# Row sums inside r's projection, kk and v in separate buffers, and the second half's tokens fetched early, in a hybrid RWKV-7 / GLA layer

## The chip, the cores and the metric

The kernel runs on one core of one Trainium2 chip. Its time is the device time of one execution in microseconds; a kernel is judged by the median of its runs. One execution is recorded by the hardware profiler, and all rows below come from that one. TensorE multiplies matrices, VectorE and GpSimd work element by element, ScalarE evaluates functions and copies, and SyncE (SP) issues the transfers.

## What is computed

One layer of a decoder is applied to 1024 prompt tokens and to 32 sample tokens (8 sequences of 4). The residual stream, 1024 wide, goes through one input projection whose columns feed two groups of heads: RWKV-7 (8 heads of 64) and gated linear attention, GLA (4 heads). Both outputs go through an output projection and a layer norm, then a gated convolutional feed-forward and a second layer norm. The part that matters here is how RWKV-7 gets its key direction:

```python
xs = pa + (prev - pa) * mu
r, k, v, w_lo, a_lo, g_lo = split_cols(xs, [A_WIDTH, A_WIDTH, A_WIDTH, A_DECAY_LORA, A_AAA_LORA, A_GATE_LORA])
...
kk = heads(k * k_k)
kk = kk * lax.rsqrt(jnp.maximum(jnp.sum(kk * kk, -1, keepdims=True), 1e-24))
k = k * (1.0 + (a - 1.0) * k_a)
...
def step(S, inp):
    r_t, d_t, k_t, v_t, kk_t, a_t = inp
    sa = jnp.einsum('bhvk,bhk->bhv', S, -kk_t)
    S = (S * d_t[:, :, None, :] + sa[..., None] * (kk_t * a_t)[:, :, None, :]
         + v_t[..., None] * k_t[:, :, None, :])
    return S, jnp.einsum('bhvk,bhk->bhv', S, r_t)
```

kk is k scaled per head to unit length. It needs the sum of squares over a head's 64 channels, which lie on partitions, so a matmul makes the sums.

## The kernel before

**Stages.** The tokens are worked in two halves: the first holds 512 prompt tokens and the 32 sample tokens (544 columns), the second 512 prompt tokens. For each half `load_x` (line 800) brings the tokens in as eight tiles of 128 tokens by 512 channels (ten in the first half), transposes them on TensorE and splits them into a high part xh and a low part xl. Every projection (`gemm`, line 231) then makes three matmuls for each of 8 blocks of channels: 24 for a block of tokens. The first half has two blocks of 272 columns, the second one of 512. The result lands in one of two PSUM banks of the pool pg ("g" in the profile), and is evicted from there. The weights are split in the same way in `win_tile` (line 220): ScalarE casts the high part (line 225), GpSimd subtracts for the low part (line 227). Raw, high and low parts have three buffers each, and a projection takes two of each.

**Pairs.** RWKV-7 works on pairs of heads, four to a half, so Q0 to Q7. `rwkv_prep` (line 847) makes a pair's factors in this order: the projection of k with the low-rank parts of decay and in-context rate between its matmuls (lines 856 to 863, 882); the squares sq of k (line 886, ScalarE); the projection of r (line 888); the row sums of sq on TensorE and their inverse root by three Newton steps on VectorE (`pair_rsqrt`, lines 889 and 264 to 292, steps in lines 282 to 286, with a copy on ScalarE in line 290); kk from k and the transposed roots (line 898); ba = kk x a on GpSimd (line 908); the scaled factors ar (lines 910, 917) and bk (lines 920, 923) on VectorE; the projection of v (line 930), evicted by ScalarE in line 778 and corrected for the previous token by VectorE in line 772. `post` (line 938) then makes the score matrices from ar and bk (matmuls of line 943, masked in line 945), transposes bk, and forms the bonus and the transposed v.

**Buffers.** The tags e1, e3 and e4 of the pool p2 have one buffer each. In a pair e1 holds in turn sw, sq and ba, and e4 holds kk and then v. The buffers of GLA (e2, gep, sg and others) lie in the pool pl; fl, the low-rank input of GLA's decay, has a buffer in p2.

**Order.** The program is written by generators that `weave` (line 187) advances by a planned TensorE time: streams (`stream_r` for RWKV-7, `stream_g` for GLA, `stream_w` for the output projection) are taken one at a time by priority, chains (`chain_p` for post, `chain_i`, `chain_c`, `chain_t` for the recurrence, `chain_g` for GLA's) are slipped in when due. Events such as "G0" (the GLA projections of the first half are issued) or "P3" (post of Q3 is issued) hold a generator back. Order of writing is a priority: the compiler then orders each engine's queue by what its own model takes to be ready, so the trace can show instructions of a queue in another order than written, and once compiled each queue runs in order. SP's transfers are such a queue too.

**Between the halves.** `stream_r` waits for "G0" and calls `load_x` for the second half. Its eight tiles go into the buffers of raw, high and low weight parts in turn (line 809), all of them issued in `load_x`; a planned pause of 3 us follows (line 815), then the transposes. `gla_f` (line 974) follows with small weights (fraw) in the raw buffers, and `half_start` (line 829) once "P3" is there. A GLA pair ends in `gla_chain` (line 632): its last steps read the buffers sg and write the output (lines 690 to 703).

Of the kernel before, what the change touches and what calls it, by code (L numbers as in the profile page):

```python
# [9 lines left out]
F32 = mybir.dt.float32  # L10
# [7 lines left out]
P = 128  # L18
# [25 lines left out]
def step_kernel(  # L44
# [8 lines left out]
    act, dve, pool, sp = nc.scalar, nc.vector, nc.gpsimd, nc.sync  # L53
# [23 lines left out]
    pe = TensorE()  # L77
# [5 lines left out]
    def rtok(t0):  # L83
        return x_prompt[0, t0:t0 + P, :] if t0 < NP else x_sample.rearrange("b t d -> (b t) d")
# [48 lines left out]
    p2 = cx.enter_context(tc.tile_pool(name="p2", bufs=1))  # L133
    px = cx.enter_context(tc.tile_pool(name="px", bufs=1))
# [52 lines left out]
    def weave(chains, streams):  # L187
        chains, streams = [Thread(c) for c in chains], [Thread(c) for c in streams]
        cur, slot = None, 0.0
        while any(t.alive for t in chains + streams):  # L190
            live = [c for c in chains if c.ready()]
            due = [c for c in live if c.due <= pe.t]
            off = [c for c in due if not c.pe]
            if off:
                off[0].step()
                continue
            if cur is None or cur.free:
                cur = min((t for t in streams if t.ready()), key=lambda t: t.prio, default=None)
            if due and (pe.t - slot >= SLOT or cur is None or not cur.ready()):
                for c in due:  # L200
                    if c.ready():
                        c.step()
                slot = pe.t
                continue
            if cur is not None and cur.ready():
                cur.step()
                continue
            due = [c.due for c in live] + [t.blocked for t in streams if isinstance(t.blocked, float)]
            assert due, [(t.alive, t.blocked) for t in chains + streams]
            pe.t = min(due)  # L210
# [77 lines left out]
    def pair_rsqrt(sq, n, *ops):  # L288
        y = rows_rsqrt([(sq, sel2, 0)], n, *ops)
        act.copy(sq[:, 0:512].rearrange("p (a c) -> p a c", c=64), y[:, 0:8].unsqueeze(2).to_broadcast([P, 8, 64]))  # L290
        return y
# [474 lines left out]
    def shifted(H, c0, xs, ws=None):  # L766
        ft = c0 // P
        ws = ws or win_tile(c0)
        mu, halo_ = col(V_MU + ft), halo[:, ft:ft + 1]

        def add_prev(out, prev):
            dve.scalar_tensor_tensor(out, prev, mu, out, ALU.mult, ALU.add)
        for s, e in H.blocks:
            ps = gtile()
            yield from gemm(ps, ws, s, e)
            ep = min(e, 512)
            m = ep - s
            act.activation(xs[:, s:e], ps[:, 0:e - s], AF.Identity, scale=omu[:, ft:ft + 1])
            add_prev(xs[:, s + 1:ep], ps[:, 0:m - 1])
            add_prev(xs[:, s:s + 1], halo_)  # L780
            dve.tensor_copy(halo_ if H.base + ep < NP else nsh[:, ft, 0:1], ps[:, m - 1:m])
            if e > 512:
                pv, xv = s3(ps[:, 512 - s:544 - s]), s3(xs[:, 512:544])
                add_prev(xv[:, :, 1:], pv[:, :, 0:NS - 1])
                add_prev(xv[:, :, 0], sst[:, ft, :])
                dve.tensor_copy(nsh[:, ft, 1:9], pv[:, :, NS - 1])
# [9 lines left out]
    def take(gen, n):  # L796
        for _, item in zip(range(n), gen):
            yield item

    def load_x(H, between=None):  # L800
        tiles = []
        for g in range(2):
            for t0 in range(0, H.n, P):
                w, i = min(P, H.n - t0), len(tiles)
                if H.sam:
                    xt = (px.tile([P, 512], F32, name="xt", tag=("wh", "wl")[i // 3], bufs=3) if i < 6 else
                          p2.tile([P, 512], F32, name="xt", tag=("e1", "e3", "e4", "fl")[i - 6]))
                else:
                    tag, bufs = (("wraw", 3), ("wh", 3), ("wl", 3))[i % 3]
                    xt = px.tile([P, 512], F32, name="xt", tag=tag, bufs=bufs)  # L810
                sp.dma_start(xt[:w, :], rtok(H.base + t0 if t0 < 512 else NP)[:, 512 * g:512 * g + 512])
                tiles.append((t0, w, g, xt))
            if between:
                between(4 * g)
        yield ("until", pe.t + 3.0)
        for i, (t0, w, g, xt) in enumerate(tiles):
            if i % 2 == 0 or i > 3 and not H.sam:
                ps = ttile()
            else:
                ps = gtile() if i < 4 else otile("og" if i % 4 == 1 else "o")  # L820
            for j in range(4):
                pe.transpose(ps[:, j * P:j * P + w], xt[:w, j * P:(j + 1) * P], ident[:w, :w])
            src = ps.rearrange("p (j t) -> p j t", j=4)[:, :, :w]
            act.copy(xh[:, 4 * g:4 * g + 4, t0:t0 + w], src)
            dve.tensor_tensor(xl[:, 4 * g:4 * g + 4, t0:t0 + w], src,
                              f(xh[:, 4 * g:4 * g + 4, t0:t0 + w]), ALU.subtract)
            yield 0.5
# [19 lines left out]
    def rwkv_prep(Q):  # L847
# [37 lines left out]
        sq = p2.tile([P, 544], F32, name="sq", tag="e1")  # L885
        act.activation(sq[:, 0:n], k[:, 0:n], AF.Square, scale=col(V_KK + p))
        rr = s1([P, 544], "r", 3)
        yield from shifted(H, pc0, rr)
        y = pair_rsqrt(sq, n, 1e-24, 0.0, ALU.max, ALU.add)
        if Q.i >= 2:  # L890
            yield ("wait", f"C{Q.i - 2}")
        Q.E = rr_.tile([P, 8, 2, 2, CH], F32, name="E", tag="E", bufs=2)
# [1 line left out]
        Q.bkT = rr_.tile([P, 8, P], F32, name="bkT", tag="bkT", bufs=2)  # L894
        Q.ar = ars[Q.i % 2]
        Q.bon = rr_.tile([P, 512], F32, name="bon", tag="bon", bufs=2)
        kk = p2.tile([P, 544], F32, name="kk", tag="e4")
        dve.scalar_tensor_tensor(kk[:, 0:512], k[:, 0:512], col(V_KK + p), pair_spread(sq), ALU.mult, ALU.mult)
        if sam:
            ps = ttile()  # L900
# [3 lines left out]
            dve.scalar_tensor_tensor(kk[:, 512:544], k[:, 512:544], col(V_KK + p), ps[:, 0:32], ALU.mult, ALU.mult)  # L904
        arp = Q.ar
        bk = rr_.tile([P, 8, 2, CH], F32, name="bk", tag="bk")
        ba = p2.tile([P, 544], F32, name="ba", tag="e1")
        pool.tensor_tensor(ba[:, 0:n], kk[:, 0:n], aa[:, 0:n], ALU.mult)
        for h in range(2):
            dve.scalar_tensor_tensor(arp[own[h], :, 0, 1 - h, :], c3(kk)[own[h]], -1.0, pp[own[h], :, 0:CH],  # L910
# [314 lines left out]
    def chain_c():  # L1225
        for Q in Qs:
            yield ("wait", f"P{Q.i}")
            yield 1.0
            rwkv_values(Q)
            yield ("wait", f"I{Q.i}")  # L1230
            if Q.i >= 2:
                yield ("wait", f"T{Q.i - 2}")
            yield ("off", 1.0)
            yield from rwkv_chunks(Q)
            yield ("done", f"C{Q.i}")

    def chain_p():
        for Q in Qs:
            yield ("wait", f"R{Q.i}")
            if Q.i >= 2:  # L1240
                yield ("wait", f"T{Q.i - 2}")
            yield max(0.0, Q.t + POST - pe.t)
            yield from Q.post
            yield ("done", f"P{Q.i}")

    def chain_i():
        for Q in Qs:
            yield ("wait", f"P{Q.i}")
            yield 3.0
            yield from rwkv_inverse(Q)  # L1250
            yield ("done", f"I{Q.i}")

    def chain_t():
        for Q in Qs:
            yield ("wait", f"C{Q.i}")
            yield from rwkv_tail(Q)
            yield ("done", f"T{Q.i}")

    def chain_g():
        for hf, H in enumerate(Hs):  # L1260
            for g in range(2):
                yield ("wait", f"Q{hf}{g}")
                yield 2.0
                yield from gla_chain(g, hf, H.st[g])
                for q in range(2):
                    if (1, 2)[q] == 2 * hf + g:
                        yield ("wait", "P3")
                        yield ("wait", "C7" if hf * g else "P3")
                        yield from rwkv_samples(q)
                yield ("done", f"D{hf}{g}")  # L1270

    def stream_r():
        for hf, H in enumerate(Hs):
            if hf:
                yield ("wait", "G0")
                yield from load_x(H)
                yield ("done", "X1")
            yield ("wait", "lock")
            yield from half_start(H, *([] if hf else [ws0]))
            yield ("free", "lock")  # L1280
            if hf == 0:
                constants()
                yield ("done", "X0")
            for Q in Qs[4 * hf:4 * hf + 4]:
                yield ("prio", R_PRIO[Q.i])
                yield ("wait", "lock")
                yield from rwkv_prep(Q)
                yield ("free", "lock")
# [254 lines left out]
    def wpost(t0, w, xz):  # L1543
        x1, xo = (W.xa, t0) if t0 < 512 else (W.xb, t0 - 512)
        for g in range(2):
# [9 lines left out]
                act.activation(W.yc[:, 4 * g:4 * g + 4, t0 - T0:t0 - T0 + w], pv, AF.Copy, scale=ALPHA)  # L1555
            yield 0.5

    weave([chain_g(), chain_p(), chain_c(), chain_i(), chain_t()],
          [stream_r(), delay_posts(stream_w()), stream_g()])
    xa, xb, cvec, sct, f0 = W.xa, W.xb, W.cvec, W.sct, W.f0  # L1560
    wop.close()
# [195 lines left out]
```

## Time and profile before

| | us |
|---|---|
| three timed runs | 1653.04, 1675.87, 1679.36 |
| their median | 1675.87 |
| the profiled execution | 1657.51 |
| its span, first to last instruction | 1655.8 |

The span is what the rows count from: a start of 282.49 is 282.49 us after the first instruction. "Busy" of an engine is the time in which it ran an instruction. In a row of the timeline the bracket tells how long the engine had been idle before it and which instruction ended the wait.

### The profile page before, as it was taken

How to read it: one execution, taken by the hardware profiler on the slowest of the kernel's cores; microseconds unless marked ns; L12 is line 12 of the kernel's file. 1: busy time of each engine (PE TensorE's matmuls, PEld its weight loads, DVE VectorE, ACT ScalarE, POOL GpSimd, SP SyncE). 2: the span in 40 equal slices, each digit the busy share in tenths (PEclk: the TensorE clock that was granted, in tenths of full speed). 3: DMA queues.
4: the chain of work that ended last, by engine and by line, in shares of the span. 5: the costliest groups of instructions: out<-in, count | busy, mean ns of one | idle time of the engine just before them, and what ended most of it. 6: DMA issues, size and time to landing. Idle time of an engine off the chain costs nothing.

```text
span 1655.8 us, 28781 instructions
## 1 busy us (share of the span) xinstructions
PE 1570.6 (95%) x11728; PEld 1324.3 (80%) x11728; DVE 945.6 (57%) x2083; ACT 529.4 (32%) x986; POOL 358.7 (22%) x583
## 2 busy tenths in 40 slices
PE   7899889889999999998999999999999999999997
PEld 6788777766676667666878898898988889888996
DVE  4566567676787767536774444544445443454348
ACT  4453443435444435344223131221202212121222
POOL 5434424323444343331000000000000000000005
PEclk9999998989999989999999999999999999999999
DMA  4122122131211013232313020210202112021102
GB/s 140 47 65 65 39 65 71 34 85 33 59 39 46 27 46 103 79 105 87 100 43 102 26 64 27 64 52 27 64 25 65 45 34 64 14 77 43 48 27 106
DMA packets 138572, 97.36 MB, mean 59 GB/s; under 512 B 15963, under 2 KB 127003, under 8 KB 138440
## 3 DMA queue, kind: packets, MB, share of 16 engines
q1 hardware_dynamic: 138440, 95.52, 19.5%
q8 instruction: 92, 1.51, 0.4%
q14 instruction: 40, 0.33, 0.1%
HBM read 84.36 MB, written 11.15 MB: 58 GB/s over the span
## 4 chain that ended last, share of the span: by engine, by line
PE 60%; DVE 5%; issue 2%; ACT 1%; POOL 1%; DMA 1%; DVEq 0%; POOLq 0%; ACTq 0%
PE g L71 26%; PE t L71 18%; PE dn L71 13%; PE t L75 1%; PE opso L71 1%; PE sps L71 1%; PE opsog L71 1%; DVE st L1485 0%; PE up L71 0%; DVE rst L285 0%; DVE yt L1665 0%; DVE ya L1642 0%; DVE tm L327 0%; DVE yt L1666 0%; PE rp L71 0%
## 5 line engine op out<-in xcount | busy, mean ns | idle before, releaser
L71 PE MATMUL g<-xh,wh 128*128 128x272 f32 (+1 forms) x624 | 221.3, 355 | 9.5 <-DVE sg L1094 3.5
L71 PE MATMUL g<-xh,wl 128*128 128x272 f32 (+1 forms) x624 | 215.2, 345 | 3.2 <-POOL wl L227 3.2
L71 PE MATMUL g<-xl,wh 128*128 128x272 f32 (+1 forms) x624 | 216.2, 347 | 0.0
L1458 DVE TENSOR_TENSOR wlu<-wraw,whu 128x1024 fp32r<-128x1024 f32 x45 | 55.1, 1224 | 229.2 <-ACT whu L1453 220.2
L227 POOL TENSOR_TENSOR wl<-wraw,wh 128x512 fp32r<-128x512 f32 x104 | 136.3, 1313 | 168.8 <-ACT wh L225 154.2
L1607 POOL COPY ncv<-gp 128x2 f32<-128x2 f32 x22 | 20.6, 936 | 610.1 <-ACT gp L1599 610.1
L71 PEld LDWEIGHTS g<-xh,wh 128*128 128x128 f32 x624 | 122.0, 196 | 22.6 <-issue 7.0
L71 PEld LDWEIGHTS g<-xh,wl 128*128 128x128 f32 x624 | 122.2, 196 | 11.4 <-POOL wl L227 3.7
L71 PE MATMUL g<-xb,whu 128*128 128x288 f32 (+1 forms) x688 | 130.9, 288 | 0.0
L71 PE MATMUL t<-xb,whu 128*128 128x256 f32 (+1 forms) x688 | 130.5, 288 | 0.0
L71 PEld LDWEIGHTS g<-xl,wh 128*128 128x128 f32 x624 | 122.3, 196 | 9.0 <-issue 3.3
L71 PEld LDWEIGHTS t<-xb,whu 128*128 128x128 f32 x688 | 109.7, 189 | 1.8
L71 PEld LDWEIGHTS g<-xb,whu 128*128 128x128 f32 x688 | 109.7, 189 | 1.8
L71 PE MATMUL t<-xa,whu 128*128 128x512 f32 x352 | 110.2, 394 | 0.0
L225 ACT CAST wh<-wraw 128x512 fp32r<-128x512 f32 x104 | 64.0, 618 | 131.1 <-PE g L71 79.3
L71 PE MATMUL g<-xa,whu 128*128 128x512 f32 x336 | 105.6, 395 | 0.0
L1642 DVE TENSOR_TENSOR ya<-ya,dn 128x512 f32<-128x512 f32 x108 | 73.3, 684 | 53.7 <-PE dn L71 53.7
L71 PE MATMUL g<-xb,wlu 128*128 128x256 f32 (+1 forms) x344 | 99.3, 289 | 0.0
L71 PE MATMUL t<-xb,wlu 128*128 128x256 f32 (+1 forms) x344 | 99.2, 288 | 0.0
L71 PE MATMUL dn<-whd,hh 128*128 128x512 f32 x240 | 94.9, 395 | 0.0
L71 PE MATMUL dn<-wld,hh 128*128 128x512 f32 x240 | 94.6, 394 | 0.0
L71 PE MATMUL dn<-whd,hl 128*128 128x512 f32 x240 | 94.3, 393 | 0.0
(515 smaller groups left out, 3518.9 us busy)
## 6 DMA issues: line engine op xcount, KB each, us to landing
wraw<-in_w_in_dram SPq DMA_DIRECT2D x104, 256.0 KB
wraw<-in_w_up_dram SPq DMA_DIRECT2D x43, 512.0 KB
wraw<-in_w_down_dram SPq DMA_DIRECT2D x22, 512.0 KB
xt<-in_x_prompt_dram SPq DMA_DIRECT2D x16, 256.0 KB
woraw<-in_w_out_dram SPq DMA_DIRECT2D x7, 512.0 KB
ob<-od SPq DMA_DIRECT2D x7, 512.0 KB
out_dram<-yt SPq DMA_DIRECT2D x6, 512.0 KB
ya<-in_x_prompt_dram SPq DMA_DIRECT2D x5, 512.0 KB
```

Of the source, the lines that this page charges most:

```text
L71: return nc.tensor.matmul(out, lhsT, rhs, **kw)
L75: return nc.tensor.transpose(out, in_, idn)
L225: act.copy(wh, raw)
L227: pool.tensor_tensor(wl, raw, f(wh), ALU.subtract)
L1458: dve.tensor_tensor(wl, raw, f(wh), ALU.subtract)
L1607: pool.tensor_copy(ncv[:, i, 0:2], gp[:, 1024:1026])
L1642: dve.tensor_tensor(y[:, cs], y[:, cs], ps, ALU.add)
```

## The change

Three things are changed. In `rwkv_prep` the projection of r is interrupted after 24 matmuls (12 in the second half), the row sums and their inverse root are issued there, and the projection goes on. kk moves to e1 and ba is made in place in aa's buffer, so that e4 holds v alone. A new chain `fetch_x` waits until the first half's second GLA pair is finished (a new event "F01"), and issues the loads of the first five x tiles of the second half into e2, gep, both sg and fl; `load_x` then issues only the last three, all into raw weight buffers, after waiting for the fetch to be issued ("XP"), and leaves out the planned pause.

```diff
+    def fetch_x():
+        yield ("wait", "F01")
+        H1.xt = []
+        for i in range(5):
+            tag, bufs = (("e2", 1), ("gep", 1), ("sg", 2), ("sg", 2), ("fl", 1))[i]
+            xt = (p2 if i == 4 else pl).tile([P, 512], F32, name="xt", tag=tag, bufs=bufs)
+            sp.dma_start(xt, rtok(512 + P * (i % 4))[:, 512 * (i // 4):512 * (i // 4) + 512])
+            H1.xt.append(xt)
+        yield ("done", "XP")
+
     def load_x(H, between=None):
@@
+                elif i < 5:
+                    tiles.append((t0, w, g, H.xt[i]))
+                    continue
                 else:
-                    tag, bufs = (("wraw", 3), ("wh", 3), ("wl", 3))[i % 3]
-                    xt = px.tile([P, 512], F32, name="xt", tag=tag, bufs=bufs)
+                    xt = px.tile([P, 512], F32, name="xt", tag="wraw", bufs=3)
@@
-        yield ("until", pe.t + 3.0)
+        if H.sam:
+            yield ("until", pe.t + 3.0)
@@
         rr = s1([P, 544], "r", 3)
-        yield from shifted(H, pc0, rr)
+        main = shifted(H, pc0, rr)
+        yield from take(main, 24 if sam else 12)
         y = pair_rsqrt(sq, n, 1e-24, 0.0, ALU.max, ALU.add)
+        yield from main
@@
-        kk = p2.tile([P, 544], F32, name="kk", tag="e4")
+        kk = p2.tile([P, 544], F32, name="kk", tag="e1")
@@
-        ba = p2.tile([P, 544], F32, name="ba", tag="e1")
+        ba = aa
@@
                 yield from gla_chain(g, hf, H.st[g])
+                yield ("done", f"F{hf}{g}")
@@
                 yield ("wait", "G0")
+                yield ("wait", "XP")
                 yield from load_x(H)
@@
-    weave([chain_g(), chain_p(), chain_c(), chain_i(), chain_t()],
+    weave([chain_g(), chain_p(), chain_c(), chain_i(), chain_t(), fetch_x()],
```

## Rows read from the trace of the kernel before

**Rows 1.** The page: busy time of each engine, share of the span, instructions.
```profile
PE 1570.6 (95%) x11728; PEld 1324.3 (80%) x11728; DVE 945.6 (57%) x2083; ACT 529.4 (32%) x986; POOL 358.7 (22%) x583
```

**Rows 2.** Stretches: length, busy by engine (instructions), granted clock, DMA share, GB/s.
```profile
57.00:66.00 9.00, 5.23 (x25) 3.98 (x24) 7.90 (x18) 1.48 (x3) 3.74 (x5) 0.71 0.22 58
...
168.00:178.00 10.00, 6.33 (x33) 4.88 (x32) 7.92 (x21) 1.49 (x3) 4.09 (x7) 0.83 0.26 79
...
283.50:298.50 15.00, 11.57 (x101) 10.48 (x101) 13.14 (x40) 2.71 (x5) 8.33 (x11) 1.00 0.26 76
...
335.30:349.50 14.20, 9.43 (x72) 8.46 (x71) 14.04 (x50) 2.56 (x5) 2.94 (x3) 0.93 0.38 114
...
353.00:362.00 9.00, 9.00 (x37) 5.95 (x37) 4.93 (x9) 4.96 (x11) 3.30 (x5) 0.74 0.33 89
```

**Rows 3.** Timeline of TensorE: start, length, instruction, idle time before and its end.
```profile
60.12 0.43 PE L71 MATMUL rp<-srw,ar 128*128 128x64 f32 x2 [1.64 <-DVE ar L910]
62.69 0.76 PE L71 MATMUL t<-ar,bk 128*128 128x256 f32 x1 [2.13 <-DVE bk L920]
...
173.60 1.19 PE L71 MATMUL t<-ar,bk 128*128 128x256 f32 x2 [3.67 <-DVE gosb L695]
...
298.48 0.67 PE L71 MATMUL t<-ar,bk 128*128 128x256 f32 x2 [3.43 <-DVE gosb L695]
...
348.67 1.08 PE L75 MATMUL g<-ident,xt 128*128 128x128 f32 x4 [4.16 <-issue]
...
487.43 1.12 PE L75 MATMUL t<-ident,sq 128*128 128x128 f32 x4 [2.93 <-ACT sq L290]
...
585.44 0.74 PE L71 MATMUL opso<-E,UV 128*64 128x64 f32 x18 [1.94 <-POOL UV L454]
```

**Rows 4.** Timeline of the third pair (Q2), all engines, by engine.
```profile
282.49 1.23 PE L71 MATMUL t<-sel,sq 128*128 128x64 f32 x10
...
294.02 0.29 PE L71 MATMUL g<-xl,wh 128*128 128x272 f32 x1
294.14 0.29 PE L71 MATMUL g<-xh,wl 128*128 128x272 f32 x1
...
291.72 0.75 DVE L898 SCALAR_TENSOR_TENSOR kk<-k,vec,t 128x512 f32<-128x512 f32 x1 [0.40 <-PE t L75]
...
292.54 2.43 DVE L910 SCALAR_TENSOR_TENSOR ar<-kk,pp 64x512 f32<-64x512 f32 x2
...
295.11 2.35 DVE L920 TENSOR_TENSOR bk<-ba,cum 64x512 f32<-64x512 f32 x2
...
297.59 0.74 DVE L695 SCALAR_TENSOR_TENSOR gosb<-t,hng,sg 128x512 f32<-128x512 f32 x1
...
295.29 0.87 ACT L778 ACTIVATE v<-g,omu 128x272 f32<-128x272 f32 x2
...
295.38 1.54 POOL L227 TENSOR_TENSOR wl<-wraw,wh 128x512 fp32r<-128x512 f32 x1
```

**Rows 5.** Timeline of TensorE: first and last of r's last 24 matmuls, third pair.
```profile
277.89 0.43 PE L71 MATMUL g<-xh,wh 128*128 128x272 f32 x1
...
282.28 0.37 PE L71 MATMUL g<-xh,wl 128*128 128x272 f32 x1
```

**Rows 6.** The tile rst: min/median/max of a Newton step; then the fifth pair's timeline.
```profile
L284 DVE SCALAR_TENSOR_TENSOR rst<-rst x60: 148/166/1247, 52.9 to 769.6; 128x8 f32<-128x8 f32 x42, 128x10 f32<-128x10 f32 x12, 128x9 f32<-128x9 f32 x6
...
430.07 1.28 POOL L227 TENSOR_TENSOR wl<-wraw,wh 128x512 fp32r<-128x512 f32 x1
430.18 1.20 DVE L284 SCALAR_TENSOR_TENSOR rst<-rst 128x8 f32<-128x8 f32 x1
```

**Rows 7.** Timelines of SP and TensorE around the loads of the second half.
```profile
292.60 4.71 SPq L217 DMA_DIRECT2D wraw<-in_w_in_dram  x2
...
341.40 0.29 PE L71 MATMUL g<-xh,wl 128*128 128x272 f32 x1
...
352.18 0.60 PE L71 MATMUL g<-xh,fwh 128*32 128x512 f32 x1 [0.72 <-ACT xh L824]
```

## The prediction

> **What bounds the kernel now.** I read the page first for the whole, then the stretches, then the timeline of TensorE, then one hole of it on all engines. On the page TensorE is busy for 1570.6 us, 95% of the span, VectorE for 945.6, 57% [rows 1]: this is a kernel bound by TensorE, and a change pays only where TensorE stands idle or runs at the lower clock. The profiled execution took 1657.5 us, 1.7 more than its span of 1655.8. Everything that the change touches lies before 755 us.
>
> In the timeline of TensorE the idle times with the largest numbers behind a pair's v projection are of one kind [rows 3]: 1.64 and 2.13 us at the first pair, 3.67 at the second, 3.43 at the third, 4.16 at the fourth, and in the second half 2.93 at the sixth and 1.94 at the eighth. The reader is to see what ends them: a product made from kk (ar, bk), an instruction queued on VectorE behind such products (gosb, line 695), or nothing named ("issue") where a PSUM bank was missing.
>
> The third pair shows the mechanism [rows 4]. The row sums of k squared begin on TensorE at 282.49, after the whole of r's projection. Their inverse root takes VectorE and ScalarE until kk can be made at 291.72, ar from 292.54 to 294.97, and only then, at 295.29, does ScalarE evict v, because v is to lie in kk's buffer and kk's readers must be through. Until v is evicted both banks of the projections are full, so no further projection can start, and the scores of this pair need bk, which ends at 297.46. TensorE waits until 298.48. So two things end last in turn: the chain from the row sums to bk, and the bank that v holds.
>
> After these holes the clock is low: the granted share is 0.71 from 57 to 66, 0.83 from 168 to 178, 0.93 from 335.3 to 349.5 and 0.74 from 353 to 362 [rows 2]. With two levels, full and half, that is 2 x (1 - share) x length of half clock: 5.2, 3.4, 2.0 and 4.7 us. A matmul of 272 columns took 0.43 us in such a stretch and 0.29 at the full level [rows 4, 5].
>
> **The change part by part.** *Row sums amid r's projection.* No instruction is added. The ten row-sum matmuls (eight in the second half) and what hangs on them are issued after 24 of 48 matmuls, in the second half after 12 of 24. In the third pair the first and the last of those 24 start at 277.89 and 282.28 and the sums begin at 282.49 [rows 4, 5]: the chain starts 4.6 us earlier. The square of k must be there by then; it needs only the end of k's projection. Where it is late, TensorE's queue stands in front of the sums, and the rest of r's projection behind them.
>
> *Buffers of kk and v apart.* kk takes the place of its own squares (e1), ba that of aa, v alone keeps e4. Same instructions, same sizes. v's eviction then waits for its projection alone: in the third pair it can come when the last matmul of v is through, 294.4, for the first block earlier still, and a bank is free for the next projection. What becomes late next is the second half of the next weights: their low part is made on GpSimd from 295.38 to 296.92 [rows 4], because it waits for a slot that v's projection still reads. The first half of those weights feeds 12 matmuls, 12 x 0.125 = 1.5 us at the spacing of the last two v matmuls [rows 4], from 294.4 to 295.9. That leaves about 1.0 us of hole. I take 1.0 at each of the four pairs of the first half.
> Sum over these: 1.64 + 2.13 + 3.67 + 3.43 + 4.16 = 15.0, less 4.0, is 11.0 us gained. The bounds of this term are 15.0 (next projection always ready) and 0 (VectorE, busy 13.14 of 15.0 and 14.04 of 14.2 us there [rows 2], keeps the banks anyway). I stand nearer to the upper end because VectorE has no work that only these holes could hold: over the span it is 57% busy [rows 1], and the Newton steps move to where r's projection runs.
>
> *Second half.* There one projection fills one bank, and the waits come from ScalarE and VectorE queues that serve the chunk chains too. Of 2.93 + 1.94 = 4.9 us I take half, 2.4; bounds 0 and 4.9.
>
> *Clock.* The four stretches hold 15.3 us of half clock. Work there takes 0.43 for 0.29, so a third of the time, 5.1 us, is given back if no hole is left. The stretches behind the two holes of the second half I put at half as much again, an estimate. Of 7.7 I take 4.2, since holes of 1 us stay; bounds 0 and 7.7.
>
> *Tokens loaded early.* Five of eight x tiles are fetched after the first half's last GLA pair into places that are then unused; three go to the weights' raw slots. The same eight transfers are issued by SP, five earlier. The fourth pair's v matmuls end at 341.7 and the transposes' hole ended on a bank, not on a transfer [rows 3, 7]; so by itself this is worth nothing (0 to 2 us), but it covers the gain above: with the bank free at 342, tiles issued at the end of v's projection would be late. It moves one thing the wrong way: the weights of the GLA decay (fraw) follow in the raw slots, and those now hold x tiles 6 to 8 instead of 1, 4 and 7. Before, the first matmul with them started at 352.18, 10.8 us behind the last of v at 341.40 [rows 7]. Without the bank's 4.16 us that would be 6.6. Now the load waits for the sixth tile's transposes; I put the five tiles ahead of it and its own at 3.7 us, and load, cast and subtraction at 3 more, both estimates from how this stretch ran before: 6.7. A tie, cost 0 (bounds 0 and 3). The planner's pause of 3 us ahead of the transposes only orders instructions; I cost it at nothing.
>
> Sum: 11.0 + 2.4 + 4.2 = 17.6 us, from 1657.5 to 1639.9.
>
> The profiled execution lies 18.4 us below the median of the three runs, 1675.87; with it, four executions are known: 1653.0, 1657.5, 1675.9, 1679.4, whose middle is 1666.7, 9.2 above the profile. A median of the changed kernel should fall around that middle less the gain: 1639.9 + 9.2 = 1649.
>
> **The rivals.**
> *VectorE takes the gain back.* The newton steps land where GpSimd splits v's weights. A step that takes 0.17 us in the median took 1.20 beside such a split, which ran for 1.28 [rows 6]. If two of them per pair meet the Newton steps, 2 x 1.03 = 2.1 us, so the chain comes 2.5 instead of 4.6 us earlier, and r's own evictions queue behind it: some 1.5 us before v's projection at four pairs. Then 6 us of the 17.6 go, and most of the clock's share, 4: gain 7.6, 1650 on the profile's execution, 1659 at the middle. For it: VectorE at 14.04 of 14.2 us around the fourth pair [rows 2]. Against: the 57% over the span [rows 1].
> The Trainium skill ("SBUF — State Buffer", section "Who interferes with whom") says that a VectorE instruction with two SBUF inputs contends with a GpSimd one that reads SBUF and that the loser is blocked for the whole instruction. The trace agrees in the rows named. If every pair lost two full splits on TensorE's path, 8 x 2 x 1.28 = 20 us, the sum would be 1660 instead of 1639.9; no row shows that they would be on the path.
> *Only the buffers act.* The row sums come no earlier on TensorE, since k's square is late or the compiled order puts them back. Then v's eviction still frees the bank, but scores wait for bk: I give it 10 us, 1647.5, 1657 at the middle.
> *Everything closes.* 15.0 + 4.9 + 7.7 = 27.6: 1630, 1639 at the middle.
> *Slower.* SP's queue is in order. If the early x loads stand in it before the raw weights issued at 292.60 [rows 7], they hold these up until the sg buffers are read by the gosb product, 297.59 + 0.74 = 298.3 [rows 4]: the third and fourth pair's weights come 5.7 us late, the half clock behind such a hole costs 1 to 2, the fraw loads behind the last x tiles up to 3; nothing else gained, it is +10: 1667.5, 1677 at the middle. It decides once a load of x is issued ahead of those weights. Against: the gosb product itself moves earlier with the kk chain, and five loads are few.
>
> **How the numbers follow.** Forecast 0.52, VectorE 0.24, buffers alone 0.10, everything 0.06, slower 0.08. The executions known scatter by 13 us to either side of their middle, more than the cases differ: the range reaches from 1639 less about 11, 1628, to the buffers' and VectorE's case plus that scatter, 1672. A measurement of this kernel tells about 2%, 33 us, from no change; the cases end between -28 and +10, so only scatter on top of the best ones passes it: faster 0.09, within 2% 0.88, slower 0.03.
>
> **What would show it.** Right: in the timeline v's evictions start within 1 us of v's last matmul; the Newton steps run before the last matmul of r; holes behind v's projection are about 1 us; the clock shares of [rows 2] rise to 0.95 or more; the x tiles' issues on SP stand before 310. Wrong: TensorE's idle time before 780 us falls by less than 8 us, or holes of 2 us and more stand between r's and v's projection, or weights are waited for around 300.

## The result and the profile after

The changed kernel took 1672.13 us (median of 20 runs, 1657.35 to 1684.53), the kernel before, on the same chip, 1658.95 (20 runs, 1650.06 to 1679.36): a ratio of 1.0077, 95% interval 1.0055 to 1.0098. The ratios, here and below, leave out executions more than 1.5% above the fastest of their kernel, so they can differ a little from the quotient of the medians. The changed kernel is slower by 0.8%, where 1649 had been forecast: the sign was wrong, and the time lies just outside the range. The profiled execution of the changed kernel took 1669.06 us, its span is 1667.3.

What was meant to happen on the engines happened. The timeline of TensorE, of ScalarE and of VectorE for the third pair of the changed kernel answers to [rows 4]:

```profile
276.26 1.78 PE L71 MATMUL t<-sel,sq 128*128 128x64 f32 x10
277.97 0.40 PE L71 MATMUL g<-xh,wh 128*128 128x272 f32 x1
...
292.52 0.70 PE L71 MATMUL t<-ar,bk 128*128 128x256 f32 x2
...
288.96 0.49 ACT L778 ACTIVATE v<-g,omu 128x272 f32<-128x272 f32 x1 [5.50 <-PE g L71]
...
281.47 0.45 DVE L284 SCALAR_TENSOR_TENSOR rst<-rst 128x10 f32<-128x10 f32 x1
...
285.30 0.74 DVE L914 SCALAR_TENSOR_TENSOR kk<-k,vec,t 128x512 f32<-128x512 f32 x1
...
289.59 1.38 DVE L936 TENSOR_TENSOR bk<-aa,cum 64x512 f32<-64x512 f32 x2
```

The row sums stand amid r's projection, kk is made while TensorE still projects, v is evicted at 288.96 on "PE g", its own projection, and the scores at 292.52 wait for nothing. The hole of 3.43 us at this pair is gone. Other holes are there now, in the timeline of TensorE of the changed kernel:

```profile
51.72 0.55 PE L75 MATMUL t<-ident,sq 128*128 128x128 f32 x3 [1.79 <-ACT sq L290]
...
61.41 0.29 PE L71 MATMUL g<-xh,fwh 128*32 128x272 f32 x1 [1.51 <-DVE halo L781]
...
166.46 0.43 PE L71 MATMUL sps<-RU,bkT 128*128 128x64 f32 x2 [2.71 <-DVE RU L448]
...
339.63 0.63 PE L75 MATMUL g<-ident,xt 128*128 128x128 f32 x4 [0.90 <-ACT xh L838]
...
353.66 0.70 PE L71 MATMUL t<-ar,bk 128*128 128x256 f32 x2 [1.74 <-DVE E L961]
...
477.76 0.66 PE L75 MATMUL t<-ident,sqo 128*128 128x128 f32 x4 [3.58 <-ACT sqo L290]
```

Of the five holes of the first half, 15.0 us, more than half comes back as waits for something else: the inverse root itself (sq), the copy of a projection's last column (halo), a step of the recurrence (RU), the masked scores of the fourth pair (E). In the second half the hole of 2.93 us gave way to one of 3.58 that ends on another norm's inverse root (sqo). The windows of both kernels, with the columns of [rows 2], show the balance. Before:

```profile
0.00:780.00 780.00, 703.84 (x6722) 561.07 (x6723) 506.03 (x1377) 337.21 (x636) 307.09 (x479) 0.95 0.23 63
780.00:1655.80 875.80, 866.73 (x5007) 763.20 (x5006) 439.60 (x706) 192.16 (x350) 51.62 (x104) 1.00 0.17 55
...
689.00:725.00 36.00, 35.39 (x251) 24.04 (x250) 12.38 (x40) 10.91 (x22) 15.14 (x26) 1.00 0.31 81
```

After:

```profile
0.00:780.00 780.00, 708.79 (x6701) 562.63 (x6702) 501.35 (x1366) 334.83 (x631) 302.63 (x477) 0.94 0.22 61
780.00:1667.30 887.30, 874.07 (x5029) 767.83 (x5027) 444.88 (x717) 194.22 (x355) 53.68 (x106) 0.99 0.18 56
...
689.00:725.00 36.00, 36.00 (x144) 22.73 (x144) 8.09 (x25) 7.30 (x16) 8.43 (x13) 0.51 0.18 50
```

Length less busy time is TensorE's idle time: up to 780 us it was 76.2 and is 71.2. That is 5.0 us less, where the prediction called itself wrong below 8. Part of it is only late: the changed kernel is by then some 10 us behind in its work, and behind 780 it idles for 13.2 us instead of 9.1. Over the whole span the idle time is 85.2 before and 84.4 after, 0.8 less, and the same 11728 matmuls keep TensorE busy for 12.3 us longer. The loss is in busy time, not in waiting.

One row shows where: from 689 to 725 TensorE is busy for 36.00 of 36.00 us at a granted clock of 0.51, where before had 1.00. That is an unbroken stretch at the half level. Two pairs of lines from the timelines of TensorE measure it. In that place the second rwkv_samples (line 493) runs its small matmuls between the projections of the last GLA pair; its last transposes of "nat" and its first of "s0t" bound it. Before, then after:

```profile
682.88 1.06 PE L75 MATMUL t<-ident,nat 128*128 128x128 f32 x4
...
692.16 0.39 PE L71 MATMUL g<-xl,wh 128*128 128x512 f32 x1
...
711.30 0.66 PE L75 MATMUL t<-ident,s0t 128*128 128x128 f32 x4
```

```profile
680.65 0.60 PE L75 MATMUL t<-ident,nat 128*128 128x128 f32 x4
...
692.70 0.63 PE L71 MATMUL g<-xl,wh 128*128 128x512 f32 x1
...
723.57 1.11 PE L75 MATMUL t<-ident,s0t 128*128 128x128 f32 x4
```

28.42 us became 42.92. The changed kernel enters this phase 2.2 us ahead and leaves it 12.3 behind; a projection matmul takes 0.63 us in it instead of 0.39.

One number is used from here on. Every execution's record has its span and its mean granted clock; with two levels, h = 2 x span x (1 - clock) is its time at the half clock. Over the 85 executions of the kernel before that ran beside the first eleven experiments, the time follows h: 1619.8 + 0.407 h, correlation 0.99, rest 1.2 us. So h, which runs from 62 to 151 us in them, carries nearly all of this kernel's scatter. Its median is 99.5 before (98 executions, those beside the twelfth among them; the twenty of the result have no clock on record) and 123.7 after. That difference, 24.2 x 0.407, is 9.8 of the 13.2 us lost.

### The profile page after: what moved, and what is told of

It is laid out like the page before. It is cut to its first block, busy times and chain, and to the rows that moved or that the text cites. A ratio compares the mean times of both kernels' runs of the same rounds, so it can differ in the third digit from the quotient of the medians.

```text
span 1667.3 us, 28766 instructions
## 1 busy us (share of the span) xinstructions
PE 1582.9 (95%) x11728; PEld 1330.5 (80%) x11728; DVE 946.2 (57%) x2083; ACT 529.1 (32%) x986; POOL 356.3 (21%) x583
## 4 chain that ended last, share of the span: by engine, by line
PE 66%; DVE 7%; issue 2%; ACT 1%; POOL 1%; DMA 1%; DVEq 0%; ACTq 0%; POOLq 0%
PE g L71 29%; PE t L71 19%; PE dn L71 12%; PE t L75 2%; PE opsog L71 1%; PE opso L71 1%; PE sps L71 1%; PE up L71 1%; DVE tm L327 1%; PE rp L71 1%; DVE rst L285 0%; DVE bk L936 0%; DVE st L1503 0%; DVE yt L1683 0%; DVE ya L1660 0%
## 5 line engine op out<-in xcount | busy, mean ns | idle before, releaser
L71 PE MATMUL g<-xh,wl 128*128 128x272 f32 (+1 forms) x624 | 219.0, 351 | 2.8 <-POOL wl L227 2.8
```

The lines of the kernel that those rows point to most:

```text
L71: return nc.tensor.matmul(out, lhsT, rhs, **kw)
```

## The experiments

**Which part brings it?** Theory A: the long stretch at the half clock, which one part's new order brings, eats the gain. B: in the second half VectorE's Newton steps stand ahead of the recurrence. C: the early tokens cost time on SP's queue. The four kernels take parts of the change.

e1_buffers:
```
-        kk = p2.tile([P, 544], F32, name="kk", tag="e4")
+        kk = p2.tile([P, 544], F32, name="kk", tag="e1")
@@
-        ba = p2.tile([P, 544], F32, name="ba", tag="e1")
+        ba = aa
```


> Only kk into e1 and ba into aa; row sums and token loads as before. Theory A (the lost time is half clock in the last GLA pair, where small sample matmuls and projections alternate, and any new order of the queue can bring it): the holes behind v's projection in the first half shrink, the eighth pair's kk comes 5 us or more earlier, and a stretch of 20 us or more of half clock stands between 680 and 730; time 1660 to 1675. Rival B (VectorE: the Newton steps ahead of the recurrence in the second half lose the time): without the moved row sums the gain of the first half stays, 1645 to 1652. Rival C (the early tokens shift the second half): also 1645 to 1652.

e2_rows:
```
-        yield from shifted(H, pc0, rr)
+        main = shifted(H, pc0, rr)
+        yield from take(main, 24 if sam else 12)
         y = pair_rsqrt(sq, n, 1e-24, 0.0, ALU.max, ALU.add)
+        yield from main
```


> Only the row sums amid r's projection; kk, ba, v and tokens as before. Theory A: the order of TensorE changes little, no long half clock after 680, holes behind v stay at 2 us or more because v waits for kk's readers; 1652 to 1660, no different from before. Rival B: the loss shows here too, 1663 to 1672. Rival C: below before by some 5 us.

e3_tokens is the changed kernel with both of these edits undone; e4_rows_buffers is the kernel before with both, so without the early tokens.

> Only the early tokens, the event and the missing pause; rwkv_prep as before. Theory A: order of TensorE nearly as before, so the clock as before; the hole of 4.16 us ahead of the transposes stays since it waits for v's bank; 1655 to 1661. Rival B: 1655 to 1661 as well. Rival C: this alone makes it slower, 1668 or more.

> The whole change without the early tokens. Theory A: as the changed kernel if the order around 680 to 730 comes out alike, 1665 to 1675, with a long stretch of half clock there. Rival B: 1665 to 1675 too, but with holes on TensorE ended by VectorE in place of a long half clock. Rival C: the loss is gone, 1645 to 1655.

Measured, with the kernel before at 1661.79 in the same batch (the phase is the one from "nat" to "s0t"):

| kernel | median us | ratio, 95% interval | median h | phase in the profile, us |
|---|---|---|---|---|
| e1_buffers | 1652.39 | 0.9962, 0.9930 to 0.9995 | 83 | 27.33 |
| e2_rows | 1667.86 | 1.0034, 1.0002 to 1.0067 | 118 | 42.79 |
| e3_tokens | 1662.83 | 1.0024, 0.9985 to 1.0062 | 100 | 27.35 |
| e4_rows_buffers | 1671.57 | 1.0051, 1.0019 to 1.0083 | 125 | 42.72 |

In these profiles the stretch comes with the row sums, alone or with the buffers, and with nothing else. So A as it was expected missed twice: it had put the stretch with the buffers (e1: 1660 to 1675) and none with the row sums (e2: 1652 to 1660). It is kept from here on in another form: the long stretch is what costs, and the row sums bring it. B's times fit e1 (within half a microsecond) and e2, so it needs a test of its own. e3 lies 2 us above what A and B gave; C's 1668 or more for the tokens alone did not come, and they can't be told from no change. The buffers alone are a small gain, and nearly all of it is clock: e1's h is 20 us below that of the kernel before beside it (103), which at 0.407 is 8 of the 9.4 us between the medians.

**Which half, and is it the clock?** The row sums amid r in one half only, then work added to the place of the stretch, then all but the row sums.

e5_rows_first (the changed kernel, row sums moved in the first half alone):
```
-        yield from take(main, 24 if sam else 12)
+        if sam:
+            yield from take(main, 24)
+        else:
+            yield from main
```


> The whole change, but with the row sums amid r's projection in the first half alone; in the second half they stand behind r's projection as before. Theory A (the changed kernel loses its gain to one long stretch at the half clock between 680 and 730 us, and the second half's order of the row sums brings it): 1645 us, 1638 to 1653; no stretch at the half clock longer than 15 us between 660 and 740, and under 100 us at the half clock in all. Theory B (in the second half the Newton steps of the row sums stand on VectorE ahead of the recurrence, and TensorE waits): also faster than the changed kernel, but the gain is seen in TensorE's idle time up to 780 us, 71.0 us in the changed kernel and then under 65, and not in the clock. If the first half's order were what brings the stretch: 1668 to 1674, as the changed kernel.

e6_rows_second is the kernel before with the edit of e2 alone, under the opposite condition (if not sam, 12).

> The kernel before with the row sums amid r's projection in the second half alone: no change of buffers, no early tokens, the first half as before. Theory A: 1668 us, 1662 to 1676, with a stretch of over 25 us at the half clock between 670 and 740. Theory B: 1662 to 1668 without such a stretch, with more idle time of TensorE than before's 72.4 us up to 780. If the first half is what brings the loss: 1656 to 1662, no stretch.

e7_fill (the changed kernel; fill() is called nine times in the second rwkv_samples, from three places; the calls are left out here):
```
+        def fill():
+            if g == 1:
+                d = ttile()
+                for _ in range(2):
+                    nc.tensor.matmul(d, xh[:, 0, 0:P], xh[:, 0, 0:512], start=True, stop=True)
```


> The changed kernel with work added: 18 matmuls of 128x128 by 512 columns, whose result nobody reads, in nine places of the second rwkv_samples, amid its small matmuls. At 0.23 us each at the full clock that is 4.1 us more work. Theory A, in which the half clock there is what costs and hangs on what TensorE does there: the stretch of 37.5 us is gone or under 12 us, and the added work makes the kernel faster: 1672 - 18.8 + 4.1 = 1657, 1650 to 1664. If the clock falls there for a reason that the order on TensorE doesn't touch, or if it isn't what costs: 1674 to 1681, the added work and up to twice as much of it, with the stretch still there.

e8_buf_tokens is the changed kernel with r's projection and the row sums in the order of before.

> The change without the row sums amid r's projection, in both halves: buffers apart and early tokens. Theory A: no long stretch between 660 and 740; the buffers' gain stands and the tokens add at most their hole of 1.5 us: 1651 us, 1645 to 1658. Theory C (the early tokens cost time by themselves, by the places that they take on SP's queue): 1657 to 1664, over the 1652 of the buffers alone.

The kernel before took 1659.28 in this batch:

| kernel | median us | ratio, 95% interval | median h | phase in the profile, us |
|---|---|---|---|---|
| e5_rows_first | 1651.84 | 0.9958, 0.9919 to 0.9996 | 76 | 47.33 |
| e6_rows_second | 1675.74 | 1.0090, 1.0060 to 1.0121 | 131 | 42.83 |
| e7_fill | 1669.32 | 1.0044, 1.0011 to 1.0076 | 100 | 33.55 |
| e8_buf_tokens | 1659.47 | 1.0021, 0.9983 to 1.0059 | 100 | 28.77 |

The windows of e6_rows_second and, below them, of e7_fill in that place:

```profile
683.00:698.00 15.00, 15.00 (x167) 11.40 (x157) 3.02 (x10) 4.25 (x11) 2.67 (x5) 0.77 0.15 49
698.00:735.00 37.00, 37.00 (x158) 23.60 (x158) 7.89 (x26) 7.03 (x15) 8.37 (x14) 0.50 0.15 43
```

```profile
680.00:700.00 20.00, 18.12 (x328) 13.25 (x327) 8.73 (x16) 8.03 (x17) 5.77 (x8) 1.00 0.24 74
700.00:720.00 20.00, 19.61 (x147) 13.21 (x145) 6.06 (x19) 4.92 (x11) 5.97 (x11) 0.98 0.13 32
```

The second half's row sums alone, on a kernel otherwise as before, cost 16 us and bring 37 us at 0.50 of the clock. B falls with it as an explanation: most of that kernel's loss is the clock, 35 us more of h than the kernel before had beside it (96), which at 0.407 are 14 of the 16.5; and TensorE's idle time up to 830 us is 77.0 in e6's profile against 76.2 in before, so the waits that B asked for are not there. With 18 full-width matmuls put amid the small ones the clock stays up until 719, the phase is 9.4 us shorter although it holds more work, and the median h falls by 24. Over the whole kernel the median falls by 2.8 us only, where A expected 15, and the intervals of the two ratios overlap; 24 x 0.41 less 2.8 would put the price of the added work at 7 us instead of 4.1. So A's price was missed, and its mechanism is borne out by the row, not by the time. e8 missed too, by 8 us: with the tokens the buffers don't keep their gain, and its time lies in C's range. Its h is 17 above that of e1, which at 0.407 is the whole of the 7 us between them; whether the tokens bring that h was not tried.

The profiled execution of e5 was the longest of its eleven, 1678.43 us. It shows that the stretch can come in the order of before as well:

```profile
680.00:700.00 20.00, 18.87 (x268) 15.99 (x268) 3.49 (x10) 4.91 (x14) 1.69 (x5) 0.58 0.05 16
700.00:720.00 20.00, 20.00 (x86) 12.77 (x86) 4.19 (x13) 1.10 (x3) 2.86 (x4) 0.50 0.11 27
```

It is a matter of how often. A high h stands for it here, although other places add to h too. Of the executions with at least 110 us of h there are 43 in 49 in the four kernels with the second half's row sums moved and nothing added (after, e2, e4, e6), 23 in 98 of the kernel before, 2 in 11 here.

**Is it the row sums or the order?** On TensorE the small opsog matmuls of the second rwkv_samples stand in two orders. In before, e1, e3, e5 and e8 they come in runs of 4, 12, 7 and 9 (each leaves two records in the trace), with the last blocks of the last pair's inverse between them; in after, e2, e4 and e6 in runs of 3, 4, 9, 4, 8 and 4, with the matmuls of its chunk chain (sps, rp, up, 64 columns each) between them, since the inverse came earlier. These are lines of TensorE around the fall of the clock in the changed kernel:

```profile
685.98 0.68 PE L71 MATMUL opsog<-s0t,ax 64*64 64x64 f32 x8
686.59 0.43 PE L71 MATMUL sps<-RU,bkT 128*128 128x64 f32 x2
686.95 1.58 PE L71 MATMUL opsog<-s0t,ax 64*64 64x64 f32 x16
688.46 0.69 PE L71 MATMUL rp<-YS,ar 128*128 128x64 f32 x2
...
692.11 0.79 PE L71 MATMUL g<-xh,wh 128*128 128x512 f32 x1
```

The clock falls in the second of these rows: it is 1.00 from 680.65 to 687 and 0.50 from 687 to 692.11, TensorE being busy all the time; its last hole ended at 673.61. Two matmuls of rp take 0.69 us at 688.46, where they took 0.33 in before at 692.39. No projection matmul runs between the transposes at 680.65 and 692.11; but neither does one between 683.1 and 691.82 in before. And the clock of before falls in this place as well, in these windows of before and, below them, of after:

```profile
680.00:690.00 10.00, 9.34 (x165) 7.73 (x157) 2.07 (x6) 3.62 (x10) 0.79 (x2) 0.83 0.08 29
690.00:700.00 10.00, 10.00 (x77) 6.82 (x77) 2.58 (x10) 1.75 (x4) 2.59 (x6) 1.00 0.10 26
```

```profile
680.00:690.00 10.00, 10.00 (x100) 8.50 (x98) 1.76 (x7) 2.48 (x7) 1.23 (x4) 0.85 0.06 18
690.00:700.00 10.00, 10.00 (x45) 6.24 (x45) 1.53 (x6) 1.13 (x3) 1.83 (x3) 0.50 0.11 26
```

Summed over windows of half a microsecond, before has 3.4 us of half clock between 681.5 and 685.5, and the clock comes back amid the small matmuls. The stretch that begins at 687 in after has 37.5 us, and the ones in the profiles of e4, e6 and e2 have 37.5, 37.5 and 37.6. In these profiles the difference is not that the clock falls but how long it stays down.

Three kernels move the inverse of the last pair later, by one number in chain_i, and a fourth does so on the kernel before:

```
-            yield 3.0
+            yield 3.0 if Q.i < 7 else 6.0
             yield from rwkv_inverse(Q)
```


> The whole change, with one number altered: the inverse of the last pair is put 6 instead of 3 us of the planner's time behind its post step, so that TensorE's order in the second rwkv_samples is again that of the kernel before (runs of 4, 12, 7 and 9 small matmuls, with the inverse's last two blocks between them; in the changed kernel 3, 4, 9, 4, 8 and 4, with the last pair's chunk chain between them). Nothing is added or left out. Theory A, now in this form: the row sums bring the long stretch only by that order. Then no stretch over 15 us at the half clock between 660 and 740, a median of 85 to 105 us at the half clock instead of 124, and 1658 us, 1650 to 1665. If the row sums in the second half cost by themselves, or the stretch doesn't hang on that order: 1668 to 1676.

e10_inverse_later has 12.0 for 6.0; e11_first_later is e5_rows_first with 12.0; e12_before_later is the kernel before with 12.0.

> As the kernel with 6 us, but 12 us behind the post step: the last pair's inverse then comes after most of the second rwkv_samples, which stands in runs of 4, 12, 12 and 4 small matmuls. Theory A gives no number of its own for a third order: if a long stretch needs the chunk chain amid these small matmuls, it is gone here too and the time is 1655 to 1665; a later end of the chunk chain, which TensorE has no other work for, would add up to 6 us. If the stretch comes back here, what brings it is not the chunk chain.

> The change with the row sums amid r's projection in the first half alone, and the last pair's inverse 12 instead of 3 us behind its post step. A candidate for a faster kernel: by theory A the chance of the long stretch falls from the 3 in 11 executions of the first-half version to none, which takes 4 to 6 us off its mean and 0 to 4 off its median of 1651.8: 1650 us, 1644 to 1656. If the third order of the small matmuls has a long stretch of its own: 1660 to 1670.

> The kernel before, with nothing of the change, and the last pair's inverse 12 instead of 3 us behind its post step. It tells what share of the fastest version's gain (1645.8 against 1660.0) is the change's and what is that one number's. If the number alone earns it, by fewer executions with a long stretch at the half clock: 1646 to 1651, and 65 to 80 us at the half clock. If the change's parts in the first half carry it: 1654 to 1661, 85 to 100 us at the half clock.

The kernel before took 1660.03 beside the first three and 1661.95 beside the last:

| kernel | median us | ratio, 95% interval | median h (range) | phase in the profile, us |
|---|---|---|---|---|
| e9_inverse_late | 1657.81 | 0.9973, 0.9937 to 1.0008 | 76 (66 to 86) | 27.40 |
| e10_inverse_later | 1660.78 | 1.0007, 0.9966 to 1.0049 | 96 (69 to 117) | 24.02 |
| e11_first_later | 1645.75 | 0.9911, 0.9870 to 0.9951 | 72 (52 to 86) | 23.92 |
| e12_before_later | 1655.69 | 0.9966, 0.9936 to 0.9996 | 98 (79 to 127) | 23.94 |

The windows of e9_inverse_late:

```profile
680.00:700.00 20.00, 19.55 (x237) 14.25 (x235) 6.47 (x19) 4.66 (x14) 5.05 (x8) 1.00 0.24 69
700.00:720.00 20.00, 19.12 (x110) 12.88 (x106) 6.18 (x21) 7.62 (x15) 9.31 (x17) 1.00 0.28 65
```

e9 holds the whole change, second half's row sums included, and differs from the changed kernel by one number. The clock is 1.00 throughout these windows, no execution reaches 110 us of h, and the median is 14.3 us below that of the changed kernel, where A had expected it (the kernel before differs by 3 us at most between the batches). So the long stretch comes by the order that the row sums led to. That is not the whole of it: A had expected this time at 85 to 105 us of h, and h is 76. At equal h e9 lies 5.7 us above the line 1619.8 + 0.407 h, and what takes these is open. e10 agrees in having no long stretch (its phase, 24.02, holds less of the last pair's chunk chain); its median h is 20 above e9's from other places, and what puts them there wasn't tried. e11 is faster than the kernel before by 0.9%, interval 0.5 to 1.3, and faster than the changed kernel. The number alone, e12, brings 0.3 of it, with times and h where the first half's parts were expected to carry the gain; that the rest is the buffers, the tokens and the first half's row sums is argued from the difference. Over all, the twelve kernels without added work lie on average between 3.3 us below and 5.7 us above the line of the kernel before, while their medians span 30 us: what tells them apart is mostly h.

## Why the prediction was wrong

*The mechanism in the first half: right. Its size, 11.0 us: mis-sized.* The chain came earlier, v was evicted on its own projection, and the holes that ended on ar, bk and gosb went. But the step "That leaves about 1.0 us of hole. I take 1.0 at each of the four pairs" looked only at the next weights. TensorE had other late work behind them, the inverse root itself at the first pair (1.79 us), the recurrence's RU at the second (2.71) and the masked scores E at the fourth (1.74), and those holes opened. What is left of the term can be read across the runs: v of the fifth pair is evicted at 442.98, 443.15, 439.09 and 436.74 us in the four profiles whose first half has neither buffers nor row sums changed (before, e3, e6, e12), and at 431.53, 441.61, 439.37, 429.30, 436.02 and 434.78 in the six with the whole change there (after, e5, e7, e9, e10, e11). Means of 440.5 and 435.4: 5.1 us earlier. TensorE's idle time up to that eviction agrees, 48.7 us on average in the four and 43.8 in the six. Part of the lead is clock, as the spread among the six shows: with 0.41 us taken off per us of half clock up to that point it is 3.4. The lead of 11 us that the profile of after has there is in good part luck.

*Second half, 2.4 us: wrong sign.* The forecast took half of the holes there. The hole at 487.43 was replaced by one of 3.58 at 477.76 that ends on another norm. From v of the fifth pair to v of the eighth TensorE's idle time is 10.4 us before and 13.3 after, 2.9 more, so the second half gave back more than half of what the first had gained. And the row sums moved there were what cost the time: 16 us in e6, most of it by the clock.

*Clock, 4.2 us given back: the step that failed.* The text read "bounds 0 and 7.7" and took the clock to follow the holes: fewer holes, less half clock. Measured, h rose by 24 us, and that cost 9.8. Where the prediction looked it was not far off: in the places of its four stretches (0.71, 0.83, 0.93 and 0.74) the changed kernel's profile has 1.00, 0.91, 1.00 and 1.00:

```profile
52.00:61.00 9.00, 7.67 (x58) 6.82 (x56) 8.70 (x19) 1.94 (x5) 5.21 (x7) 1.00 0.27 71
160.00:170.00 10.00, 7.29 (x46) 6.61 (x46) 9.76 (x20) 2.12 (x4) 6.46 (x8) 0.91 0.20 52
...
325.00:340.00 15.00, 13.22 (x149) 11.81 (x149) 14.80 (x51) 4.21 (x8) 6.65 (x9) 1.00 0.10 36
343.00:352.00 9.00, 7.57 (x34) 4.19 (x34) 8.38 (x17) 4.54 (x10) 3.23 (x4) 1.00 0.49 117
```

What it left out is half clock that does not stand behind a hole: in the stretch from 687 on TensorE is busy in every microsecond, with small matmuls and projections in turn. The rows of before did not give that away; the stretch from 353 to 362, where TensorE is busy for 9.00 of 9.00 us at 0.74, ends a low clock that began in the hole before it. (The matmul of 0.43 us by which a third of the time was reckoned stands in none of the four stretches but at 277.89, at the half level too.) What was at hand was the scatter of the four known executions, 26 us, which was taken as given; by the line it is some 65 us of half clock that came and went in one and the same program.

*The rest.* 13.2 less 9.8 leaves 3.4 us in which the changed kernel is slower at equal h, though its profile has 0.8 us less idle time; in e9 it is 5.7. Where these 3 to 6 us go is open.

*The rivals.* VectorE beside GpSimd: the Newton step at 281.47 took 0.45 us beside a split that ran from 280.61 to 281.89, the others of that pair 0.15 to 0.22. The Trainium skill ("SBUF — State Buffer", section "Who interferes with whom"), which says that the loser of such a pair is blocked, agrees with that row; as a price it was a quarter of a microsecond there. At the first pair it was a whole one, and on TensorE's path, since the copy sq that TensorE waits for at 51.72 stands behind this step:

```profile
48.83 1.28 POOL L227 TENSOR_TENSOR wl<-wraw,wh 128x512 fp32r<-128x512 f32 x1 [3.06 <-ACT wh L225]
...
49.00 1.14 DVE L285 TENSOR_TENSOR rst<-rst 128x10 f32<-128x10 f32 x1
```

So this rival took some 1 of the 1.79 us that came back there. *Only the buffers act*: the row sums did come earlier, so its condition failed; the buffers without them, e1, gained 9.4 us where 10 had been put, but by the clock. *Slower*, by SP's queue, had the right sign for a wrong reason: the early tokens alone are at 1.0024, 0.9985 to 1.0062. *The middle of four executions*, 1666.7, was 8 us over the median of the twenty runs, 1658.95. That hid part of the miss: from 1658.95 the forecast gain of 17.6 would have given 1641. That the time is only just outside the range is owed to this.

## What to carry to other kernels

Before a change of order is priced by the holes that it closes, list what is late next on every engine, and expect a good part of a hole to open again behind it. On a kernel bound by TensorE, take the granted clock of every execution beside its time, and compare the order of small and full-width matmuls before and after a change, also far behind the edit: here the edit was at a pair's row sums, the loss at the samples of the recurrence, in the last GLA pair. Six profiles with the same first half reached one and the same eviction up to 12 us apart, so a lead in one trace is to be compared with other traces of the same code.

## What was not expected of the hardware

The clock went to its half level, 1.2 of 2.4 GHz, while TensorE was busy without a gap, and stayed there for 37.5 us: 0.50 in 698 to 735 of e6, with 37.00 of 37.00 us busy, full-width matmuls of 512 columns alternating with ones of 64 columns. At the full level the same mixture ran on at 1.00 (before, 689 to 725, 35.39 of 36.00 us busy). Ahead of the fall in after TensorE had been busy for 13 us, the last 6 of them without a projection matmul. That does not make a rule: in before, TensorE ran no projection matmul from 683.1 to 691.82, and the clock, which had fallen at 681.5, rose to the full level within that time, at 685.5; and in e5's profile the long stretch came behind the order of before. The order decides how often the long stretch comes (43 of 49 executions against 23 of 98, none of 10 in e9); what in the order does it is open. And a microsecond of half clock cost 0.41 us, not the 0.5 that a busy TensorE would lose, over 85 executions of one program.
